# A two-layer trunk on one core: four kinds of store and two kinds of load change their issuing queue

## The chip, the cores and the metric

The kernel runs on one core of a Trainium2 chip. A core has TensorE (PE) for matmuls, VectorE (DVE), ScalarE (ACT) and GpSimd (POOL) for elementwise work, and SyncE (SP), which here only issues transfers. SP, ACT and POOL each have an instruction queue of their own that is worked off in order; a transfer that one of them issues moves between HBM and the on-chip memory while the queue goes on. The metric is the device time of one execution in microseconds (us), as a median of several runs.

## The reference, cut to what matters

The input `x` is 1024 positions by 1024 features in fp32. Two layers each hold a mixer and a feed-forward part. The mixer of layer 0 is a gated delta rule, that of layer 1 a retention.

```python
e = silu(c @ cond_w + cond_b)
for i in range(2):
    sh1, sc1, g1, sh2, sc2, g2 = split(e @ ada_w[i] + ada_b[i], 6)
    y = mixers[i](x * (1.0 + sc1) + sh1)          # gated delta rule, then retention
    x = layer_norm(ALPHA * x + (1.0 + g1) * y, ln_g[i, 0], ln_b[i, 0])
    gate, up = split((x * (1.0 + sc2) + sh2) @ ffn_up[i], 2)          # 1024 -> 2 x 2816
    y = (silu(causal_dwconv(gate, ffn_conv_w[i]) + ffn_conv_b[i]) * up) @ ffn_down[i]
    x = layer_norm(ALPHA * x + (1.0 + g2) * y, ln_g[i, 1], ln_b[i, 1])
```

## The kernel before, in words

Every fp32 product is made of three matmuls on rounded halves: `split` (L89, L90) has ACT copy a tile into a high part and DVE subtract it for the low part. The kernel works through these stages in time: delta rule with its projections (to about 700 us), first up projection (760 to 1160), first down projection (1160 to 1390), retention projections and core (1390 to 2070), its output projection (to 2210), second up projection (2210 to 2660) and second down projection (to the end).

The up projections work on eleven pairs of 128-column blocks, `fp` = 0 to 10, some 40 us each, with a matrix scheme that needs seven products in place of eight. For each of a pair's two items `wino` loads two weight tiles `wr` of 128 x 1024 (L1357, L1358; there are two buffers `wr`), builds differences of their halves on DVE (L1346), splits each half or difference into `wb`, and PE multiplies. ACT moves some sums off PSUM (`pc`, L1362). On the gate's result `conv_q` runs the causal convolution: an ACT copy (L1732), two DVE steps (L1737) and an ACT SiLU (L1738), into a tile `o`; then DVE multiplies by the up result (L1760). `store` (L1749) writes seven blocks per pair to `ad` in HBM: three as they are and four sums or differences, which POOL makes in place (L1768; DVE for `fp` = 0). There are 11 x 7 x 2 = 154 such stores of 256 KB. The `o` tiles are drawn from twenty half tiles `qkv`, of which the scheme holds sixteen here, so that a pair writes into the four tiles that the last pair stored from.

The down projections and retention's output projection are `proj_gen`: they read the seven blocks back as `ar` (L1425), load weight blocks as `Br` or `Bw` (`load_b`, L1458, 256 KB each, by the names "11", "21", "T1" to "T4"), split both into `ab` and `bb`, and add the residual rows `xt`, which `load_row` fetches (L296, 512 KB each; the first four rows belong to `half` 0, the last four to `half` 1). Br and ar share the `qkv` tiles. In the delta rule, `t_decay` stores eight decay matrices `Ld` of 512 KB (L842). In retention, `gain_step` writes sixteen scaled blocks `xg` of 256 KB back (L2052).

The order of each engine's queue is not the order of the code: the program is laid out by a scheduler that models when each instruction would be ready on its engine and queues them by that. `after(key)` only asks that an instruction is queued behind the one that `anchor[key]` holds. When a transfer moves to another engine, the queues of the others can thus change order too.

Of the kernel before, what the change touches and what calls it, by code (L numbers as in the profile page):

```python
# [15 lines left out]
P = 128  # L16
# [10 lines left out]
ABLK = ("11", "12", "22", "S1", "S2", "S3", "S4")  # L27
# [6 lines left out]
def trunk_kernel(ctx: ExitStack, tc, A):  # L34
    nc = tc.nc
    pe, act, dve, pool, sp = nc.tensor, nc.scalar, nc.vector, nc.gpsimd, nc.sync
# [9 lines left out]
    def tl(tag, shape, dt=F32, name=None):  # L46
        return sb.tile(shape, dt, tag=tag, name=name or tag, bufs=BUFS[tag])
# [31 lines left out]
    def flat(ap):  # L79
        return ap.rearrange("p a b -> p (a b)")  # L80

    def hs(half):
        return slice(half * HALF, (half + 1) * HALF)
# [8 lines left out]
    anchor = {}  # L92

    def after(key):
        return tc.issue_after(anchor[key].ins) if key in anchor else nullcontext()
# [84 lines left out]
    for k in range(KT):  # L180
        w = tl("hTa", [P, D], name="mvw")
# [107 lines left out]
    def build_hT(tag, xts, scale, shift, fr=range(KT)):  # L289
        return [build_one(tag, xts, scale, shift, f) for f in fr]  # L290

    def load_row(src, half, t, key=None, tag="lane"):
        xt = tl(tag, [P, D], name="xt")
        r0 = half * HALF + t * P
        with after(key), after("w" if key is None else None):
            sp.dma_start(xt, src[r0:r0 + P, :])  # L296
        return xt

    def mma(acc, t, a, w, first, last, mm):
# [91 lines left out]
    xg = [dr.tile([S, D], F32, tag=f"xg{i}", name=f"xg{i}") for i in range(3)]  # L391
# [229 lines left out]
    xt = [[tl("lane", [P, 2, HALF], name="xt") for _ in range(4)], [[None, None] for _ in range(4)]]  # L621
# [76 lines left out]
    U, DT, R, St = {}, {}, {}, {}  # L698
# [22 lines left out]
    def after_ev(*names):  # L721
        return ("ev", names)

    def emit(name, lat=0.0):
        events[name] = clk[0] + lat
# [45 lines left out]
    def take(tag, n):  # L771
        while free[tag] < n:
            yield lambda: free[tag] >= n
        free[tag] -= n
# [40 lines left out]
    Ld = dr.tile([GH, P, S], F32, tag="Ld", name="Ld")  # L815
# [17 lines left out]
    def t_decay(p):  # L833
        yield after_ev(("g",), ("DD", p - 1), ("T", p // 2 - 1))
        for h in pairs[p]:
            yield from take("aux", 1)
            U[h] = tl("aux", [P, NCH, P], name="U")
            yield from decay(h)
        yield LAT["mm"]
        for h in pairs[p]:  # L840
            act.activation(flat(U[h]), flat(U[h]), AF.Exp)
            sp.dma_start(Ld[h], flat(U[h]))  # L842
        emit(("DD", p), LAT["exp"])

    def t_path(g):
# [383 lines left out]
    c, z = "c", "z"  # L1229
# [5 lines left out]
    for p in range(4):  # L1235
        q = p & 2
# [192 lines left out]
    def proj_gen(nj, ablk, wsrc, slots, xsrc, G, final, ln_next, tag, ltags, dst, key, mm=pe.matmul, gate=None):  # L1429
# [8 lines left out]
        def keep(which, j):  # L1438
            t = slots[which]
            if t == "qkv":  # L1440
                return tl(t, [P, HALF], name="Bw")
            if j % 2 == 0:
                box[which] = tl(t, [P, 2, HALF], name="Bw")
            return box[which][:, j % 2]

        src = {"11": "11", "21": "21", "T1": "12", "T2": "22", "T3": "11", "T4": "21"}

        def load_b(bn, j):
            if bn not in src:
                return  # L1450
            if bn == "11":
                t = C[j] = keep("c", j)
            elif bn == "T2":
                t = X[j] = keep("x", j)
            else:
                t = R[bn, j] = tl("qkv", [P, HALF], name="Br")
            m = src[bn]
            anchor["w"] = sp.dma_start(t, wsrc[(m[1] == "2") * 1, j][:, hs((m[0] == "2") * 1)])  # L1458

        def bblk(bn, j):  # L1460
            if bn in ("11", "22"):
# [32 lines left out]
        def xload(half, t):  # L1494
            if half and t < 2:
                x = load_row(xsrc, half, t, tag="xT")
            elif half and final:
                x = two("auh", F32, "xt")
                r0 = HALF + t * P
                for hf in range(2):  # L1500
                    with after("w"):
                        sp.dma_start(x[hf], xsrc[r0:r0 + P, hs(hf)])
            else:
                x = load_row(xsrc, half, t)
            xts[half].append(x)
            stats[half].append(tl("st", [P, 2, 6]))

# [100 lines left out]
        for p, (an, bn, fin, side, fresh) in enumerate(prods):  # L1608
# [8 lines left out]
            for j in range(nj):  # L1617
# [4 lines left out]
                if (p, j) in ready:  # L1622
                    a, w = ready.pop((p, j))
                else:
                    a, w = ops(an, bn, j, not gate and p < (7 if final else 5))
# [3 lines left out]
                if not gate and p == 2 and j % 2 == 0 and j < 8:  # L1629
                    xload(0, j // 2)  # L1630
                if final and p == 3 and j % 2 == 0 and j < 8:
                    xload(1, j // 2)
# [48 lines left out]
    def layer_tail(i, mix, wout, xsrc, x_mid, x_out, ln_next, final):  # L1681
# [25 lines left out]
        ad = dr.tile([NF // 2, 7, P, HALF], F32, tag=f"ad{i}", name=f"ad{i}")  # L1707
# [4 lines left out]
        def pair_items(fp):  # L1712
            g, o = [], {}

            def gate_start():
                g.extend(tl("lane", [P, D], name="g") for _ in range(2))

                def gate(q, a, b):
                    dst = g[q // 2][:, hs(q % 2)]
                    if b is None:  # L1720
                        act.activation(dst, a, AF.Copy)
                    else:
                        dve.tensor_tensor(dst, a, b, ALU.add)
                return gate

            def conv_q(q):
                f, hf = 2 * fp + q // 2, q % 2
                gv = g[q // 2]
                w = cw[:, 3 * f:3 * f + 3]
                t = tl("qkv", [P, HALF], name="o")  # L1730
                with after("sp") if fp == 0 else nullcontext():
                    act.activation(t, gv[:, hs(hf)], AF.Copy, scale=w[:, 2:3])  # L1732
                for j in (1, 2):
                    c0 = HALF if hf else j
                    c1 = HALF * (hf + 1)
                    tv = t[:, c0 - HALF * hf:]
                    dve.scalar_tensor_tensor(tv, gv[:, c0 - j:c1 - j], w[:, 2 - j:3 - j], tv, ALU.mult, ALU.add)  # L1737
                act.activation(t, t, AF.Silu, bias=cb[:, f:f + 1])  # L1738
                o[q] = t

            def conv():
                for q in (1, 3, 0, 2) if fp == 0 else range(4):
                    if fp < 2:
                        late.append(lambda q=q: conv_q(q))
                    else:
                        conv_q(q)

            def store(nm, q):
                sp.dma_start(ad[fp, ABLK.index(nm)], o[q])  # L1749

            def up_start():
                seen = []

                def gated(q, a, b):
                    while q not in o:
                        late.pop(0)()
                    c = a
                    if b is not None:
                        dve.tensor_tensor(c, a, b, ALU.add)
                    dve.tensor_tensor(o[q], o[q], c, ALU.mult)  # L1760
                    if q != 1:
                        store({0: "11", 2: "12", 3: "22"}[q], q)
                    seen.append(q)
                    if len(seen) == 4:
                        for d, x, y, op, nm in ((1, 1, 3, ALU.add, "S1"), (0, 1, 0, ALU.subtract, "S2"),
                                                (2, 2, 0, ALU.subtract, "S4"), (3, 3, 0, ALU.subtract, "S3")):
                            def one(d=d, x=x, y=y, op=op, nm=nm):
                                (dve if fp == 0 else pool).tensor_tensor(o[d], o[x], o[y], op)  # L1768
                                store(nm, d)
                            if fp == 0:  # L1770
                                late.append(one)
                            else:
                                one()
                return gated

            return [(up[4 * fp], up[4 * fp + 2], gate_start, conv), (up[4 * fp + 1], up[4 * fp + 3], up_start, None)]
# [93 lines left out]
    for t in range(4):  # L1870
        x = tl("cv", [P, 516], name="xlo")[:, 0:HALF]
        r0 = HALF + t * P
# [174 lines left out]
    def gain_step(m):  # L2047
        if gx:
            x, c, rs, gb = gx.pop()
            pool.tensor_tensor(x, x, gb[0], ALU.mult)  # L2050
            pool.tensor_tensor(x, x, gb[1], ALU.add)
            sp.dma_start(xg[0][rs, hs(c)], x)  # L2052
        if m < 2 * NCH:
            c, r = divmod(m, NCH)
            if r == 0:
                gbs.append([tl("auh", [P, HALF], name="gb") for _ in range(2)])
                for t, nm in zip(gbs[-1], ("ln_g", "ln_b")):
                    sp.dma_start(t, A[nm][1:2, hs(c)].to_broadcast([P, HALF]))
            rs = slice(r * P, r * P + P)
            x = tl("lane", [P, HALF], name="xg")  # L2060
            sp.dma_start(x, xs[1][rs, hs(c)])
            gx.append((x, c, rs, gbs[-1]))
# [111 lines left out]
```

## Time and profile before

| | |
|---|---|
| median of 3 runs | 2893.8 us (2892.51 to 2897.38) |
| profiled execution | 2895.86 us, span 2894.1 us |
| mean granted TensorE clock | 0.989 |
| bytes moved | 465.30 MB, mean 161 GB/s |
| SP issues | 1278 transfers before, 1052 after |
| POOL issues | 33 transfers before, about 250 after |

A group's row in the profile names the line, the engine, the operation, the tiles written and read, their shape and the count, then busy time, mean time of one, and idle time of the engine just before with what ended it. A row of waits reads: who waited, for which engine and line, us in total, how often, and the longest. A row of the chain of waits gives start, length, engine, tile and line. SPq and PEld are SP's queue and PE's weight loads.

### The profile page before, as it was taken

To read this page: it belongs to the slowest core of one execution; us is meant where nothing else is said; L and a number is where in the kernel's file an instruction comes from. 1 tells how busy PE (TensorE), PEld (TensorE's weight loads), DVE (VectorE), ACT (ScalarE), POOL (GpSimd) and SP (SyncE) were. 2 spreads that over 40 slices of the span, in tenths; PEclk is the share of its full clock that TensorE was granted. 3 is DMA by queue.
4 is the path that set the end of the run, shared out by engine and by line. 5 is a ranking of instruction groups with operands and counts; after the bars stand their busy time and mean duration, and the time that the engine had idled before them with its cause. 6 is when DMAs were issued, how large, how long until landed. Compare 5 with 4: busy or idle time off the path is not lost.

```text
span 2894.1 us, 38921 instructions
## 1 busy us (share of the span) xinstructions
PE 2796.1 (97%) x13594; PEld 2287.9 (79%) x13594; DVE 2180.7 (75%) x3874; ACT 1295.6 (45%) x2387; POOL 487.1 (17%) x509
## 2 busy tenths in 40 slices
PE   8999999999999999999999999999999999999997
PEld 6787888877788778887888887777777788888886
DVE  5787688676788888868687656666688887777779
ACT  4663465344654444545333342222244644444543
POOL 0311221000023233000000002333201023332001
PEclk9999999999999999999999999999999999999999
DMA  7223243164254555855343364665754154434853
GB/s 277 88 95 121 91 137 99 52 240 153 95 189 164 193 182 171 295 154 189 126 148 120 120 200 151 198 207 172 245 195 146 62 197 138 142 129 164 289 182 117
DMA packets 252884, 465.30 MB, mean 161 GB/s; under 512 B 24144, under 2 KB 77776, under 8 KB 252688
## 3 DMA queue, kind: packets, MB, share of 16 engines
q1 hardware_dynamic: 218560, 408.02, 42.8%
q10 hardware_dynamic: 31488, 46.15, 4.3%
q0 software_dynamic: 2640, 8.65, 0.8%
q8 instruction: 107, 1.75, 0.3%
q14 instruction: 89, 0.73, 0.1%
HBM read 346.86 MB, written 115.87 MB: 160 GB/s over the span
## 4 chain that ended last, share of the span: by engine, by line
PE 54%; DVE 23%; DMA 12%; ACT 5%; issue 5%; POOL 1%; SPq 0%; ACTq 0%; DVEq 0%; POOLq 0%
PE acc L716 8%; PE acc L1292 5%; PE acc L1592 4%; PE acc L110 4%; PE acc L111 4%; PE acc L112 4%; PE sc L716 4%; DMA mvw<-in_ada_w 3%; PE sc L1292 3%; PE mm L716 2%; DVE o L1737 2%; DVE wb L90 2%; DMA wr<-in_ffn_up 2%; DVE qkv L490 2%; DVE mm L1346 2%
## 5 line engine op out<-in xcount | busy, mean ns | idle before, releaser
L716 PE MATMUL acc<-hT,wh 128*128 128x512 f32 x960 | 301.3, 396 | 0.0
L1592 PE MATMUL acc<-bb,ab 128*128 128x512 f32 x984 | 232.5, 396 | 7.1 <-DVE ab L90 3.7
L89 ACT ACTIVATE ab<-ar 128x512 fp32r<-128x512 f32 x210 | 131.1, 630 | 222.8 <-PE mm L303 49.8
L1592 PEld LDWEIGHTS acc<-bb,ab 128*128 128x128 f32 x984 | 185.6, 190 | 49.0 <-DVE bb L90 4.1
L716 PEld LDWEIGHTS acc<-hT,wh 128*128 128x128 f32 x960 | 183.7, 191 | 36.1
L90 DVE TENSOR_TENSOR ab<-ar,ab 128x512 fp32r<-128x512 f32 x210 | 147.8, 710 | 83.0 <-ACT ab L89 83.0
L1292 PE MATMUL acc<-T,wb 128*128 128x512 f32 x840 | 202.0, 390 | 0.4 <-DVE wb L90 0.4
L716 PE MATMUL acc<-hT,wl 128*128 128x512 f32 x480 | 197.9, 412 | 3.5 <-ACT sq L509 2.4
L89 ACT ACTIVATE wb<-mm 128x512 fp32r<-128x512 f32 x216 | 124.3, 597 | 169.5 <-DVE mm L1346 155.2
L1292 PEld LDWEIGHTS acc<-T,wb 128*128 128x128 f32 x840 | 157.6, 188 | 33.7 <-ACT o L1738 1.2
L90 DVE TENSOR_TENSOR wl<-wr,wh 128x1024 fp32r<-128x1024 f32 x98 | 124.6, 1272 | 76.5 <-ACT wh L89 72.8
L89 ACT ACTIVATE wh<-wr 128x1024 fp32r<-128x1024 f32 x98 | 103.6, 1060 | 138.3 <-PE acc L716 53.5
L90 DVE TENSOR_TENSOR wb<-wr,wb 128x512 fp32r<-128x512 f32 x162 | 115.8, 716 | 62.9 <-ACT wb L89 62.9
L1768 POOL TENSOR_TENSOR o<-o 128x512 f32<-128x512 f32 x80 | 113.4, 1426 | 267.4 <-ACT pc L1362 176.3
L1737 DVE SCALAR_TENSOR_TENSOR o<-g,vc,o 128x512 f32<-128x512 f32 (+2 forms) x176 | 149.6, 860 | 8.6 <-ACT o L1732 7.4
L90 DVE TENSOR_TENSOR wb<-mm,wb 128x512 fp32r<-128x512 f32 x216 | 145.2, 685 | 7.6 <-ACT wb L89 7.6
L89 ACT ACTIVATE wb<-wr 128x512 fp32r<-128x512 f32 x162 | 101.1, 626 | 92.7 <-PE acc L1292 27.9
L1346 DVE TENSOR_TENSOR mm<-wr 128x512 f32<-128x512 f32 x108 | 85.8, 794 | 74.5 <-DMA wr<-in_ffn_up 60.9
L716 PE MATMUL acc<-wh,hT 128*128 128x512 f32 x384 | 134.4, 412 | 1.8 <-DVE vv L90 1.8
L1362 ACT ACTIVATE pc<-acc 128x512 f32<-128x512 f32 x143 | 84.3, 590 | 108.7 <-PE acc L1292 63.0
L239 DVE SCALAR_TENSOR_TENSOR ada<-mvw,e,ada 128x512 f32<-128x512 f32 x140 | 106.0, 757 | 26.0 <-DMA mvw<-in_ada_w 25.7
L110 PE MATMUL acc<-T,wb 128*128 128x512 f32 x292 | 114.5, 392 | 5.2 <-DVE wb L90 5.1
(674 smaller groups left out, 7369.9 us busy)
## 6 DMA issues: line engine op xcount, KB each, us to landing
wr<-in_ffn_up SPq DMA_DIRECT2D x92, 512.0 KB, 3.9
mvw<-in_ada_w SPq DMA_DIRECT2D x80, 512.0 KB, 4.3
ad<-o SPq DMA_DIRECT2D x154, 256.0 KB, 2.3
ar<-ad SPq DMA_DIRECT2D x154, 256.0 KB, 3.8
Br<-in_ffn_down SPq DMA_DIRECT2D x88, 256.0 KB, 3.4
wr<-in_ret_wv SPq DMA_DIRECT2D x32, 512.0 KB, 3.6
ar<-od SPq DMA_DIRECT2D x56, 256.0 KB, 4.8
wr<-in_gdn_wqkv SPq DMA_DIRECT2D x24, 512.0 KB, 3.6
```

The lines of the kernel that those rows point to most:

```text
L89: anchor["sp"] = act.activation(dst_h, src, AF.Copy)
L90: eng.tensor_tensor(dst_l, src, dst_h, ALU.subtract)
L110: mm(acc, wl[:, k], hl[0], start=first, stop=False)
L111: mm(acc, wh[:, k], hl[1], start=False, stop=False)
L112: mm(acc, wh[:, k], hl[0], start=False, stop=last)
L239: dve.scalar_tensor_tensor(a, wr[:, kk], e[:, k:k + 1], a, ALU.mult, ALU.add)
L716: pq(pe.matmul(out, lhsT, rhs, start=start, stop=stop), cost or COST[out.shape[-1]])
L1292: return pe.matmul(*a, skip_group_check=True, **kw)
L1346: dve.tensor_tensor(t, x, y, op)
L1592: return pe.matmul(*args, skip_group_check=True, **kw)
L1737: dve.scalar_tensor_tensor(tv, gv[:, c0 - j:c1 - j], w[:, 2 - j:3 - j], tv, ALU.mult, ALU.add)
L1768: (dve if fp == 0 else pool).tensor_tensor(o[d], o[x], o[y], op)
```

## The change

Four kinds of store and two kinds of load get another issuer. The product stores `ad<-o` of both up projections and retention's `xg` stores go from SP to POOL, the `Ld` stores from SP to ACT. In the first down projection the weight blocks except "11" and "21" go from SP to POOL (43 transfers); they no longer set the anchor "w". Of the residual rows of the first down projection and of retention's output projection, the last two of `half` 1 go from SP to POOL (four transfers). All else stays on SP.

```diff
-    def load_row(src, half, t, key=None, tag="lane"):
+    def load_row(src, half, t, key=None, tag="lane", eng=sp):
...
-        with after(key), after("w" if key is None else None):
-            sp.dma_start(xt, src[r0:r0 + P, :])
+        with after(key), after("w" if key is None and eng is sp else None):
+            eng.dma_start(xt, src[r0:r0 + P, :])
...
-            sp.dma_start(Ld[h], flat(U[h]))
+            act.dma_start(Ld[h], flat(U[h]))
...
+            eng = sp if gate or final or bn in ("11", "21") else pool
...
-            anchor["w"] = sp.dma_start(t, wsrc[(m[1] == "2") * 1, j][:, hs((m[0] == "2") * 1)])
+            ld = eng.dma_start(t, wsrc[(m[1] == "2") * 1, j][:, hs((m[0] == "2") * 1)])
+            if eng is sp:
+                anchor["w"] = ld
...
-                x = load_row(xsrc, half, t)
+                x = load_row(xsrc, half, t, eng=pool if half else sp)
...
-                sp.dma_start(ad[fp, ABLK.index(nm)], o[q])
+                pool.dma_start(ad[fp, ABLK.index(nm)], o[q])
...
-            sp.dma_start(xg[0][rs, hs(c)], x)
+            pool.dma_start(xg[0][rs, hs(c)], x)
```

Below, lines of before from L1461 on carry a number that is 3 higher in the changed kernel: the conv copy L1732 is L1735 there, the conv steps L1737 are L1740, the SiLU L1738 is L1741, `store` L1749 is L1752, and L1458 is L1459.

VectorE in the pair of the first up projection that holds the load of 941.83 us, of which the prediction speaks; `wb<-mm` and `wb<-wr` are the subtractions of splits, the second one whose end frees a `wr` buffer. Before:

```order
L1346 TENSOR_TENSOR mm<-wr 128x512
L90 TENSOR_TENSOR wb<-mm,wb 128x512
L1723 TENSOR_TENSOR g<-acc,pc 128x512
L90 TENSOR_TENSOR wb<-mm,wb 128x512
L1737 SCALAR_TENSOR_TENSOR o<-g,vc,o 128x511
L1737 SCALAR_TENSOR_TENSOR o<-g,vc,o 128x510
L90 TENSOR_TENSOR wb<-wr,wb 128x512 x2
L1346 TENSOR_TENSOR mm<-wr 128x512
```

After:

```order
L1346 TENSOR_TENSOR mm<-wr 128x512
L90 TENSOR_TENSOR wb<-mm,wb 128x512
L1726 TENSOR_TENSOR g<-acc,pc 128x512
L90 TENSOR_TENSOR wb<-mm,wb 128x512
L90 TENSOR_TENSOR wb<-wr,wb 128x512
L1740 SCALAR_TENSOR_TENSOR o<-g,vc,o 128x511
L1740 SCALAR_TENSOR_TENSOR o<-g,vc,o 128x510
L90 TENSOR_TENSOR wb<-wr,wb 128x512
L1346 TENSOR_TENSOR mm<-wr 128x512
```

The first split of a half has moved ahead of the two conv steps; the second one stays behind them. ScalarE at the same place, before:

```order
L89 ACTIVATE wb<-mm 128x512 x2
L1732 ACTIVATE o<-g,vc 128x512
L1362 ACTIVATE pc<-sc 128x512
L89 ACTIVATE wb<-wr 128x512
L1738 ACTIVATE o<-o,vc 128x512
L1362 ACTIVATE pc<-acc 128x512
L89 ACTIVATE wb<-wr 128x512
```

After:

```order
L89 ACTIVATE wb<-mm 128x512 x2
L1362 ACTIVATE pc<-sc 128x512
L89 ACTIVATE wb<-wr 128x512
L1735 ACTIVATE o<-g,vc 128x512
L1362 ACTIVATE pc<-acc 128x512
L89 ACTIVATE wb<-wr 128x512
```

The conv copy has moved behind an eviction and a split, and the SiLU further down. GpSimd over one pair of the first up projection; `ad` is the store, L411 to L413 scale and store blocks of the residual. Before:

```order
L1768 TENSOR_TENSOR o<-o 128x512 x4
L411 TENSOR_TENSOR xg<-xg,gb 128x512
L412 TENSOR_TENSOR xg<-xg,gb 128x512
L413 DMA xg_161<-xg 128x512
```

After:

```order
L1752 DMA ad_6811<-o 128x512
L1771 TENSOR_TENSOR o<-o 128x512
L1752 DMA ad_6811<-o 128x512 x2
L1771 TENSOR_TENSOR o<-o 128x512
L1752 DMA ad_6811<-o 128x512
L1771 TENSOR_TENSOR o<-o 128x512 x2
L1752 DMA ad_6811<-o 128x512 x2
L411 TENSOR_TENSOR xg<-xg,gb 128x512
L412 TENSOR_TENSOR xg<-xg,gb 128x512
L413 DMA xg_161<-xg 128x512
```

Stores now stand between GpSimd's four steps. In the first down projection SP's queue around the two rows of `half` 1, before:

```order
L1425 DMA ar<-ad_6811 128x512
L1458 DMA Br<-in_ffn_down 128x512
L1425 DMA ar<-ad_6811 128x512
L1458 DMA Br<-in_ffn_down 128x512
L296 DMA xt<-xg_161 128x1024 x2
L1425 DMA ar<-ad_6811 128x512
L1458 DMA Br<-in_ffn_down 128x512
```

After:

```order
L1459 DMA Br<-in_ffn_down 128x512
L1425 DMA ar<-ad_6811 128x512 x12
L296 DMA xt<-xg_161 128x1024 x2
L1425 DMA ar<-ad_6811 128x512 x13
```

The Br loads that alternated with ar are gone from SP's queue; they stand in GpSimd's, fifteen of them in a row, behind the last stores of the up projection.

## The prediction

> **What bounds the kernel now.** I read the page first, then busy time by stage, then what TensorE (PE) and SyncE's queue (SPq) wait for in each stage, and the chain of waits around PE's stops. The page's engines:
>
> ```profile
> span 2894.1 us, 38921 instructions
> PE 2796.1 (97%) x13594; PEld 2287.9 (79%) x13594; DVE 2180.7 (75%) x3874; ACT 1295.6 (45%) x2387; POOL 487.1 (17%) x509
> ```
>
> PE is busy 97%: 2894.1 - 2796.1 = 98 us is all that can go without less PE work. The profiled execution took 2895.9 us (span 2894.1 and 1.8 around it), 0.07% above the median 2893.8 of the runs; I make the sum on its span and subtract from the median. About 0.2% of it, 5.8 us, is what a measurement here can tell from no change. Busy time by stage (columns PE, PEld, DVE, ACT, POOL, then granted clock, DMA share, GB/s; the stages: delta rule, first up projection, first down projection, second up projection):
>
> ```profile
> 0.00:700.00 700.00, 658.47 (x4158) 558.90 (x4159) 513.08 (x1183) 357.65 (x744) 115.03 (x175) 0.98 0.40 137
> 760.00:1160.00 400.00, 392.25 (x1724) 319.54 (x1725) 340.35 (x524) 193.46 (x379) 106.84 (x84) 1.00 0.50 171
> 1160.00:1390.00 230.00, 225.05 (x990) 184.61 (x989) 175.29 (x289) 114.63 (x197) 11.52 (x10) 0.99 0.62 208
> 2210.00:2660.00 450.00, 441.67 (x1939) 359.69 (x1938) 353.57 (x534) 216.15 (x364) 110.96 (x89) 0.99 0.40 135
> ```
>
> The change can reach PE's idle 400 - 392.3 = 7.7 us in the first up projection, 5.0 in the first down projection, 8.3 in the second up projection; the delta rule has the most, 41.5. What SPq waits for at the edited lines, over the span:
>
> ```profile
> SPq L1749 <- DVE o L1760: 215.9, 51, 9.7
> SPq L842 <- ACT U L841: 75.8, 8, 14.3
> SPq L1749 <- POOL o L1768: 57.8, 57, 3.7
> SPq L2052 <- POOL xg L2051: 43.3, 16, 6.3
> ```
>
> Together 393 us of a queue that stands still for a store, with loads behind it. That looks like much, but it only counts where such a load is what PE waits for. What PE waits for, in the first up projection, in the first down projection, and in the second up projection:
>
> ```profile
> PE acc L110 <- DVE wb L90: 5.1, 4, 1.5
> PE sc L110 <- DVE wb L90: 0.7, 2, 0.4
> ...
> PE acc L1592 <- DVE bb L90: 3.3, 1, 3.3
> ...
> PE acc L110 <- DVE wl L90: 4.2, 2, 3.2
> PE acc L1292 <- DVE wb L90: 1.0, 2, 0.8
> ```
>
> In the delta rule the longest behind the start is on ScalarE, so no store of the change ends it:
>
> ```profile
> PE acc L719 <- ACT oq L488: 5.3, 1, 5.3
> ```
>
> **The change, part by part.** *The seven product stores of a column pair (L1749, 154 in all) go from SP to POOL.* The chain up to one of the four stops on `wb` of L110, and ScalarE's queue at the same place:
>
> ```profile
> 938.05 0.61 DVE g L1723
> ...
> 938.74 0.73 ACT o L1732
> ...
> 939.50 0.93 DVE o L1737
> ...
> 941.11 0.70 DVE wb L90
> ...
> 941.83 5.80 DMA wr<-in_ffn_up
> 947.65 0.70 DVE mm L1346
> ```
>
> ```profile
> 939.37 0.57 ACT L1362 ACTIVATE pc<-sc 128x512 f32<-128x512 f32 x1
> 939.84 0.62 ACT L89 ACTIVATE wb<-wr 128x512 fp32r<-128x512 f32 x1
> ```
>
> The weight load of 941.83 was issued the moment its buffer came free: the split `wb<-wr` (ACT L89, then DVE L90) ended at 941.11 + 0.70 = 941.81. So SP's wait for stores does not delay it: freeing SP by itself is worth nothing here. But the split ran late: ahead of it stood the first conv copy (ACT, 0.73) and two conv steps (DVE, from 939.50 to 941.11). The new order puts the split ahead of the copy and of the two steps. DVE has `g` until 938.66 and one more split of 0.70 before it, until 939.4; ACT's half, without the copy ahead, is done 0.73 earlier, at 939.84 + 0.62 - 0.73 = 939.7. So DVE's half ends at about 939.7 + 0.7 = 940.4 in place of 941.81: some 1.4 us earlier. The four stops are 5.1 / 4 = 1.3 us on average, 1.5 at most. The DVE work behind the load stays the same, so an earlier load reaches PE nearly whole: I take 5.8 us (5.1 + 0.7) as gone, with 0 and 7.7 as ends. What is late next there: the load itself, 5.80 us, since DVE is busy 85% of this stage.
>
> What POOL pays: its issues are longer than SP's, and between them stand its own steps.
>
> ```profile
> L413 POOL DMA_DIRECT2D xg<-xg x32: 580/580/759, 837.2 to 2631.0; - x32
> ...
> DMA to landing us min/median/max: 2.3/2.3/5.5
> ...
> L1749 SPq DMA_DIRECT2D ad<-o x154: 319/320/1307, 790.2 to 2690.3; - x154
> ...
> DMA to landing us min/median/max: 2.0/2.3/6.2
> ...
> L1768 POOL TENSOR_TENSOR o<-o 128x512 f32<-128x512 f32 x36 | 51.2, 1432 | 91.7 <-ACT pc L1362 88.5 <-DMA ad<-o 1.6
> ```
>
> Seven stores at 0.58 add 4.1 us to POOL per pair. The stage's 400 us hold about ten pairs, so POOL's 106.8 us are 10.7 of 40 per pair: it goes to 15 of 40, no bound. A store lands 0 to 0.3 us later (medians 2.3 against 2.3, minima 2.3 against 2.0). It now stands behind POOL's own steps and POOL waits for VectorE's `o`, up to 9.7 us, with L1768's steps queued behind; who waits for that is the conv copy L1735 (before: L1732), which writes an `o` tile that the last pair stored from. That copy is moved behind a split (0.62 us) and an eviction (0.57), so 0.62 + 0.57 = 1.2 us of lateness is covered. I charge nothing, and take the end in the rival below. In the trace POOL's issues are steady: 32 of L413 lie at 580 ns median, 759 at most, in stages where DVE is busy 340.35 / 400 = 85% and 353.57 / 450 = 79%. The Trainium skill, "SBUF — State Buffer", section "SBUF: two separate sides", in its box on VectorE blocking a DMA, says that GpSimd cannot write descriptors while VectorE holds the shared port pair, and gives 620 ns alone against some 3100 beside such a step; by that, an estimate, a store comes up to 2.5 us later, past the cover of 1.2, and rival B would be the result. By that rule L413's issues should scatter up to microseconds, and the trace does not agree.
>
> *The same stores in the second up projection:* the same move; what can go is the 1.0 us on `wb` of L1292. I take 1.0, ends 0 and 2.
>
> *First down projection: 43 weight blocks on POOL, the rest on SP.* The chain to its stop of 3.3 us, and SP's queue there:
>
> ```profile
> 1307.62 4.39 DMA ar<-ad
> ...
> 1312.77 2.79 DMA Br<-in_ffn_down
> ...
> 1316.97 3.18 DMA Br<-in_ffn_down
> ```
>
> ```profile
> 1307.62 0.32 SPq L1425 DMA_DIRECT2D ar<-ad  x1
> 1312.77 0.33 SPq L1458 DMA_DIRECT2D Br<-in_ffn_down  x1
> 1313.20 0.86 SPq L296 DMA_DIRECT2D xt<-xg  x2
> ```
>
> Loads go out as buffers come free: the one of 1312.77 had its tile released at that moment. On POOL each issue is 0.26 us longer (580 - 320) and lands up to 0.3 later, so two steps on the chain cost 2 x 0.3 to 0.6 = 0.6 to 1.1 us. Against this, SP stood in that wait from 1307.94 to 1312.77, and behind it were two residual rows of 512 KB (1313.20), which then shared the engines with both Br loads; now they are free to go in the pause. Two windows of this stage, and one from 2230:
>
> ```profile
> 1310.00:1330.00 20.00, 16.71 (x71) 13.43 (x70) 14.31 (x25) 4.48 (x8) 0.00 (x0) 0.96 0.41 132
> 1370.00:1390.00 20.00, 20.00 (x85) 16.42 (x84) 14.87 (x25) 3.42 (x4) 0.56 (x1) 0.93 0.43 152
> 2230.00:2245.00 15.00, 11.81 (x40) 9.17 (x39) 7.67 (x14) 3.23 (x4) 1.94 (x2) 0.77 0.39 144
> ```
>
> The granted clock is below 1 there (0.96, 0.93), which costs 0.04 x 20 + 0.07 x 20 = 2.2 us beside the 3.3 idle. The stage's ends are thus -5.5 (both gone) and +3 (1.1 more of stop, and the 2.2 of clock nearly once more); the two are opposed and I see no reason to prefer one, so I take 0.
>
> *Two late residual rows of each of two projections (L296) on POOL.* In the first down projection they are needed long after. Before the second up projection they are on the chain:
>
> ```profile
> 2223.94 4.44 DMA xt<-xg
> ```
>
> What lies behind it is the 3.2 us stop on `wl` and a clock of 0.77 over 15 us. Two issues at 0.58 in place of 0.86 / 2 = 0.43 and up to 0.3 in landing: 0 to +0.6; I take +0.5, since the landing is the larger part and nothing covers it.
>
> *Ld stores on ACT (L842), retention's xg stores on POOL (L2052).* Eight issues, at the 0.32 of SP above, are 2.6 us on an ACT busy 51% in that stage; SP gets 75.8 us of waiting back, but the PE stops there are ACT's own. Sixteen issues at 0.58 are 9.3 us on POOL, which is busy 17% of the span; SP gets 43.3 back. I take 0 for both, ends -2 and +2.
>
> **Sum:** -5.8 - 1.0 + 0 + 0.5 + 0 = -6.3 us: 2893.8 - 6.3 = 2887.5, which I round to 2887.
>
> **The rivals.** *A, nothing measurable.* The wr load takes 5.8 us however early it starts, since stores and loads now crowd together, and the splits that are earlier meet the same data. For: the bytes are unchanged and the chain says wr, not SP. Against: DMA share is 0.50, so room is there. Then 0 to -3: 2892. The Trainium skill, "DMA: Bandwidth & Descriptors", section "Issuing engines are not separate DMA queues", says the same in general: DMAs of every issuer share 16 engines, and several issuers save only issue time. By that rule A is the result.
>
> *B, slower: the conv copy waits for POOL's queue.* In order, ACT stops at L1735 until the store of the last pair has been issued by POOL, and behind it stand all splits of the weights. It decides when the first stores of a pair come more than the 1.2 us of cover later than on SP; one POOL step of L1768 (1432 ns) ahead of one would do. With 11 pairs in each up projection, 20 of them behind another, and half of 1.2 us each reaching PE: 20 x 0.6 = 12, and nothing gained: 2893.8 + 12 = 2906, from 2900 on for a part of the pairs. For: SP's waits show POOL as releaser at 57 of the stores, so they do stand close behind POOL's steps. Against: POOL is idle 73% of that stage.
>
> *C, a larger gain.* The 3.3 us stop of the first down projection and the clock behind it go: 2887.5 - 5.5 = 2882. For: the pause in SP's issues from 1307.94 to 1312.77. Against: the tiles, not SP, release the Br loads.
>
> **How the numbers follow.** Forecast 0.45 (2883 to 2892), A 0.17, B 0.23, C 0.15. Faster by over 5.8 us: C 0.15 and 0.29 of the forecast's 0.45: 0.44. Within 5.8 (0.2%): the other 0.16, A's 0.14, B's 0.02: 0.32. Slower: B 0.21 and A 0.03: 0.24. The range reaches down to C with 4 us of unknown in the delta rule and retention (2877) and up to B with half of its pairs struck, 2900, and 3 of the down projection (2903).
>
> **What would show it.** Right: PE's waits on `wb` L90 in the first up projection under 2 us, the wr load issued before 941 in the same pair, SPq with no wait at the stores. Wrong: ACT waiting at L1735 for a DMA of POOL; POOL issues well over 0.6 us; PE idle over 8 us in 1160 to 1390; a clock below 0.7 in the 15 us after 2230.

## The result, and the profile after

The changed kernel took 2908.0 us (median of 6 runs, 2901.0 to 2910.7) against 2893.2 of the kernel before beside it: a ratio of 1.0042, interval 1.0027 to 1.0056. In a second comparison it was 1.0040 (1.0021 to 1.0058). By the ratio it is slower by about 12 us, and its median lies 5 us beyond the upper end of the forecast range; the forecast had been 6 us faster. Its profiled execution took 2908.6 us. The page's head and engines:

```profile
span 2906.8 us, 38823 instructions
PE 2798.1 (96%) x13594; PEld 2285.8 (79%) x13594; DVE 2206.8 (76%) x3874; ACT 1294.3 (45%) x2387; POOL 602.4 (21%) x727
```

PE's work is the same. VectorE, with the same 3874 instructions, is busy 26.1 us longer (2206.8 - 2180.7): some of its steps have become slower. By stage, for the first up projection and the second one (to 2660):

```profile
760.00:1160.00 400.00, 392.15 (x1721) 318.04 (x1720) 349.69 (x523) 193.57 (x382) 139.74 (x154) 1.00 0.51 170
...
2210.00:2660.00 450.00, 436.60 (x1913) 353.84 (x1912) 356.28 (x525) 210.74 (x355) 147.66 (x161) 0.99 0.40 134
```

What SP waited for, in the lines that answer to those of before (no wait stands at the stores of L1752 and L2055, or at L842), before and then after:

```profile
SPq L1358 <- DVE wb L90: 85.9, 50, 5.1
```

```profile
SPq L1358 <- DVE wb L90: 217.9, 51, 6.8
```

SP is free of the stores, as intended, and waits at the weight loads instead: these need a buffer that a split releases. PE's waits in the first up projection and the second one:

```profile
PE acc L110 <- DVE wb L90: 4.1, 4, 1.6
PE sc L110 <- DVE wb L90: 1.6, 2, 1.3
...
PE sc L1292 <- DVE ada L239: 2.5, 1, 2.5
PE acc L1292 <- ACT pc L1362: 1.6, 3, 0.5
```

The 5.8 us that should have gone are still 5.7 (4.1 + 1.6), and in the second up projection a stop of 2.5 us is new. Which of VectorE's steps got slower shows when shapes are kept apart: first the splits `wb<-wr` of the second up projection before, then after, then splits and `ada` steps of the first up projection before, then after.

```profile
L90 DVE TENSOR_TENSOR wb<-wr,wb 128x512 fp32r<-128x512 f32 x60 | 42.3, 706 | 17.3 <-ACT wb L89 17.3
```

```profile
L90 DVE TENSOR_TENSOR wb<-wr,wb 128x512 fp32r<-128x512 f32 x59 | 53.2, 905 | 17.5 <-ACT wb L89 17.5
```

```profile
L90 DVE TENSOR_TENSOR wb<-wr,wb 128x512 fp32r<-128x512 f32 x59 | 43.9, 746 | 11.0 <-ACT wb L89 11.0
L239 DVE SCALAR_TENSOR_TENSOR ada<-mvw,e,ada 128x512 f32<-128x512 f32 x56 | 43.1, 770 | 0.0
```

```profile
L90 DVE TENSOR_TENSOR wb<-wr,wb 128x512 fp32r<-128x512 f32 x59 | 57.4, 975 | 10.1 <-ACT wb L89 10.1
L239 DVE SCALAR_TENSOR_TENSOR ada<-mvw,e,ada 128x512 f32<-128x512 f32 x56 | 49.6, 886 | 0.1
```

The new stop of 2.5 us in the chain of waits, then GpSimd at that place:

```profile
2374.62 0.63 ACT wb L89
...
2375.28 2.72 DVE wb L90
...
2378.02 6.33 DMA wr<-in_ffn_up
```

```profile
2372.72 1.30 POOL L1771 TENSOR_TENSOR o<-o 128x512 f32<-128x512 f32 x1
2374.32 0.56 POOL L1752 DMA_DIRECT2D ad<-o  x1 [0.30 <-POOL o L1771]
2374.90 2.53 POOL L1771 TENSOR_TENSOR o<-o 128x512 f32<-128x512 f32 x2
```

The split starts at 2375.28, inside two sums that GpSimd works back to back from 2374.90 to 2377.43, and it ends at 2378.00, when they are over: 2.72 us in place of 0.70. The weight load that waits for its buffer goes out at 2378.02, two microseconds late. The chains at two of the stops of about 0.5 us behind it begin in the same way:

```profile
2456.27 2.44 DVE wb L90
2458.73 4.20 DMA wr<-in_ffn_up
...
2572.97 1.85 DVE wb L90
2574.83 4.07 DMA wr<-in_ffn_up
```

Each load leaves when a stretched split ends. In the first up projection three stops, at 882.5, 923.3 and 1083.3, hold 4.5 of the 5.7 us, and their chains begin so as well, with splits of 2.59, 2.85 and 2.73 us; the first:

```profile
865.53 2.59 DVE wb L90
...
868.14 4.26 DMA wr<-in_ffn_up
```

To compare stages over kernels whose clocks and starts differ, the table gives the time between the same two matmuls of PE's queue (by their number in the queue), those that start at 770, 1160, 1290, 1390, 2200, 2250 and 2660 us in the kernel before. Kernels whose code is alike in a stage scatter there by 3 us in the first up projection (389.3 to 392.3) and by 0.8 in the second (409.4 to 410.2).

| kernel | first up 770-1160 | first down 1290-1390 | 2200-2250 | second up 2250-2660 | ratio to before |
|---|---|---|---|---|---|
| before | 390.0 | 100.1 | 49.8 | 410.2 | |
| changed | 390.6 | 96.9 | 50.5 | 415.6 | 1.0042 |
| changed, again | 392.3 | 95.9 | 50.5 | 416.3 | 1.0040 |
| e1 product stores alone | 390.0 | 97.5 | 45.5 | 415.2 | 1.0007 |
| e2 Ld alone | 389.3 | 98.8 | 48.7 | 409.4 | 0.9997 |
| e3 down blocks and rows alone | 392.3 | 96.3 | 47.6 | 409.9 | 0.9987 |
| e4 xg alone | 389.7 | 97.2 | 45.5 | 409.7 | 0.9991 |
| e6 all but the product stores | 391.4 | 97.0 | 47.6 | 409.4 | 0.9995 |
| e7 changed, sums on VectorE | 380.0 | 96.1 | 49.2 | 408.0 | 0.9975 |
| e7b before, sums on VectorE | 385.0 | 101.1 | 49.7 | 408.2 | 0.9974 |
| e11 e7 with fills on GpSimd | 379.9 | 99.3 | 50.5 | 414.2 | 0.9994 |
| e12 the best | 380.4 | 96.5 | 45.3 | 408.7 | 0.9943 |
| e13 changed, rows on SyncE | 391.8 | 97.3 | 48.6 | 413.2 | 1.0029 |
| e8 S stores on SyncE | 393.2 | 95.6 | 46.8 | 409.2 | 0.9997 |

The four stages do not hold the whole loss: from before to changed they add up to 3.5 us, of 12.7 between the two profiled executions. Counted in the same way, the stretch up to 770 goes from 770.1 to 774.9, but the five kernels that keep before's code in the delta rule and are not before itself take 773.2 to 778.9 there, so nothing can be read from it. The stretch from 1390 to 2200 goes from 810.0 to 812.5 and, in the repeat, 813.2; the others take 806.6 to 811.5, and no run shows whether the change costs something there.

### The profile page after: what moved, and what is told of

The parts are those of the page before. It is cut to its first block, busy times and chain, and to the rows that moved or that the text cites. A ratio compares the mean times of both kernels' runs of the same rounds, so it can differ in the third digit from the quotient of the medians.

```text
span 2906.8 us, 38823 instructions
## 1 busy us (share of the span) xinstructions
PE 2798.1 (96%) x13594; PEld 2285.8 (79%) x13594; DVE 2206.8 (76%) x3874; ACT 1294.3 (45%) x2387; POOL 602.4 (21%) x727
## 4 chain that ended last, share of the span: by engine, by line
PE 56%; DVE 21%; DMA 10%; issue 7%; ACT 5%; POOL 1%; SPq 0%; ACTq 0%; DVEq 0%; POOLq 0%
PE acc L716 8%; PE acc L1292 6%; PE acc L110 5%; PE acc L111 5%; PE acc L112 5%; PE sc L716 3%; PE sc L1292 3%; PE mm L716 3%; DVE wb L90 2%; DMA wr<-in_ffn_up 2%; DVE qkv L490 2%; PE acc L1595 2%; DMA mvw<-in_ada_w 2%; PE sc L110 2%; PE sc L111 2%
## 5 line engine op out<-in xcount | busy, mean ns | idle before, releaser
L1595 PEld LDWEIGHTS acc<-bb,ab 128*128 128x128 f32 x984 | 183.2, 188 | 47.3 <-DVE ab L90 2.8
L90 DVE TENSOR_TENSOR wb<-wr,wb 128x512 fp32r<-128x512 f32 x162 | 140.8, 871 | 62.0 <-ACT wb L89 62.0
L1752 POOL DMA_DIRECT2D ad<-o x154 | 84.4, 549 | 415.4 <-DVE o L1763 397.8
L1740 DVE SCALAR_TENSOR_TENSOR o<-g,vc,o 128x512 f32<-128x512 f32 (+2 forms) x176 | 136.0, 783 | 9.7 <-ACT o L1735 8.2
L239 DVE SCALAR_TENSOR_TENSOR ada<-mvw,e,ada 128x512 f32<-128x512 f32 x140 | 116.1, 829 | 25.0 <-DMA mvw<-in_ada_w 24.5
L1346 DVE TENSOR_TENSOR mm<-wr 128x512 f32<-128x512 f32 x108 | 81.5, 755 | 62.9 <-DMA wr<-in_ffn_up 49.7
L110 PE MATMUL acc<-T,wb 128*128 128x512 f32 x292 | 114.7, 393 | 4.7 <-DVE wb L90 4.6
```

The source lines that it names most:

```text
L90: eng.tensor_tensor(dst_l, src, dst_h, ALU.subtract)
L110: mm(acc, wl[:, k], hl[0], start=first, stop=False)
L239: dve.scalar_tensor_tensor(a, wr[:, kk], e[:, k:k + 1], a, ALU.mult, ALU.add)
L1595: return pe.matmul(*args, skip_group_check=True, **kw)
L1752: pool.dma_start(ad[fp, ABLK.index(nm)], o[q])
```

## The experiments

**Each part alone.** The edits are those of the change's diff, one at a time.

> Only the 154 product stores go to GpSimd; all else as before. Theory 1 (the loss sits in the up projections: stores between GpSimd's sums push these onto VectorE's splits, and ScalarE's conv copy waits for stores): +6 to +8 us, 2899 to 2901, with L90 wb<-wr at a mean near 0.9 us in both up projections in place of 0.75 and 0.71. Theory 2 (the loss sits in the delta rule, by ScalarE issuing the Ld stores, and in retention): 0 to +2 us. The forecast on record, for this part alone: -7.

Measured: 1.0007 (0.9994 to 1.0019). The second up projection takes 415.2 us, 5 more than before, with splits at a mean of 903 ns; the first takes 390.0. So the product stores carry the loss of the second up projection, and none that shows in the first. The total is lower than expected because 4.3 us come back in 2200 to 2250, for a reason of its own: PE's queue there has two orders. In one (before, changed, e2, e7, e7b, e11, e13) the last transposes stand eleven matmuls later in PE's queue, and the stage takes 48.6 to 50.5 us; in the other (e1, e3, e4, e6, e8, e12) 45.3 to 47.6. Which one the scheduler picks can change with an edit elsewhere.

> Only the eight Ld stores go to ScalarE. Theory 1: 0 to +2 us (the +5 us that the changed kernel's trace has in the delta rule is mostly order by chance). Theory 2: +4 to +5 us, all before 650 us.

Measured: 0.9997 (0.9981 to 1.0012). No cost that these runs could tell.

> Only the 43 weight blocks of the first down projection and the four late residual rows go to GpSimd. Theory 1: -3 us in 1280 to 1390 (the trace of the changed kernel gains 3 there) and up to +0.7 at the rows before the second up projection: 2891. Theory 2 says the same of this part; a third theory, that every transfer on GpSimd's queue costs time, says +1 to +3.

Measured: 0.9987 (0.9973 to 1.0002). 1290 to 1390 is 96.3 us. (The blocks are 44 by the trace, 33 into `Br` and 11 into `Bw`, not 43.) Kernels with the blocks on SyncE have 97.2 to 101.1 there, those with them on GpSimd 95.6 to 99.3: means 98.9 and 96.8, so some 2 us gained. No cost of GpSimd's queue as such.

> Only retention's sixteen xg stores go to GpSimd. Theory 1: 0 to +1 us. Theory 2: +2 to +3 us between 1750 and 2080.

Measured: 0.9991 (0.9978 to 1.0003), with the favourable order at 2200 (45.5). The rest is within the scatter.

**The changed kernel again, and without the product stores.**

> The changed kernel again, on the chip of the other experiments. Compared at the same granted clock, the parts alone measured +5.9 (product stores), +1.0 (Ld), -0.9 (down blocks and rows), -1.0 (xg): if the parts add, +5 us; if the parts act on each other, +10 as in the first comparison.

Measured: 1.0040 (1.0021 to 1.0058): as at first. The parts alone add to -0.2% by their ratios, partly because three of them (e1, e3, e4) fell into the favourable order at 2200, worth 2 to 4 us each, and the whole did not.

```diff
-                pool.dma_start(ad[fp, ABLK.index(nm)], o[q])
+                sp.dma_start(ad[fp, ABLK.index(nm)], o[q])
```

> The changed kernel with the 154 product stores back on SyncE. If the product stores are the cost: -3 to +1 us against before, and 409.5 us for the second up projection (before 410.2, changed kernel 415.6). If other parts or their interplay hold half of it: +4 to +5.

Measured: 0.9995 (0.9979 to 1.0010), second up projection 409.4. With the 154 product stores back on SyncE the loss is gone, and the other parts are worth about nothing together. Of the 13 us between this kernel and the changed one, the second up projection holds 6 to 7 and the other order at 2200 holds 2.8; 3 to 4 lie between 1390 and 2200, unexplained.

**Taking GpSimd's sums away.**

```diff
-                                (dve if fp == 0 else pool).tensor_tensor(o[d], o[x], o[y], op)
+                                dve.tensor_tensor(o[d], o[x], o[y], op)
```

> The changed kernel with GpSimd's four sums per pair (L1771) on VectorE, so that only stores and the xg steps are left on GpSimd there. VectorE gets 4 x 0.69 = 2.8 us per pair more. Theory 1 (the cost is VectorE's split that stands beside GpSimd's sums): the splits wb<-wr are back at about 0.70 us mean in the second up projection, from 0.91, and this kernel differs from the one with the same sums on VectorE and stores on SyncE by under 2 us in the second up projection. Rival (the cost is the in-order queue of GpSimd: ScalarE's conv copy waits for stores): the difference stays at 5 us.

> The kernel before with GpSimd's four sums per pair on VectorE, stores on SyncE: the control for the run beside it. Both theories: the splits at 0.70 us; the second up projection between 409 (no collisions left) and 416 (VectorE loaded by 2.8 us more per pair).

Measured: 0.9975 (0.9963 to 0.9988) and 0.9974 (0.9961 to 0.9988): both faster than before, though VectorE got 80 more steps. In the second up projection they are alike, 408.0 and 408.2, so the stores on GpSimd cost nothing there once the sums are elsewhere. In the first up projection stores on GpSimd gain 5 us (380.0 against 385.0): 3.1 of it at two places, the rest in steps of 0.3 us or less, and no run shows the cause. It is not the new order of VectorE's queue: in the first up projection the split stands ahead of both conv steps in nine pairs of the changed kernel, but in one of e7 and none of e7b. In the second it does in eight of the changed kernel, seven of e7 and none of e7b: there, with the sums away, the new order neither costs nor gains. The splits and PE's waits of the kernel with the stores on GpSimd, in the first up projection:

```profile
L90 DVE TENSOR_TENSOR wb<-wr,wb 128x512 fp32r<-128x512 f32 x60 | 42.2, 705 | 15.2 <-ACT wb L89 15.1
PE acc L1292 <- DVE wb L90: 1.2, 2, 1.0
```

All stops of L110 on `wb` are gone. But two things went with the sums: the stretched splits, and the lateness of stores behind sums in GpSimd's queue.

**Lateness without stretching.**

```diff
-                                (dve if fp == 0 else pool).tensor_tensor(o[d], o[x], o[y], op)
+                                anchor["sum"] = dve.tensor_tensor(o[d], o[x], o[y], op)
+                                if fp:
+                                    with after("sum"):
+                                        for _ in range(2):
+                                            pool.memset(tl("t2", [P, HALF]), 0.0)
```

> As the run with the sums on VectorE and stores on GpSimd, but GpSimd gets two fills of a spare 128x512 tile per sum as a stand-in, which read no memory; they do nothing for the result. Theory 1 (GpSimd steps that read memory beside VectorE's splits are the cost): if the trace shows the splits at 0.70 us beside the fills, the second up projection stays at 408 to 409 us. Rival (a busy in-order GpSimd queue, whose stores come late for ScalarE's conv copy): it goes back to 413 to 416 with splits at 0.70. If the fills lengthen the splits too, the run cannot tell the two apart.

Measured: 0.9994 (0.9983 to 1.0005). The splits stay short (699 ns in the second up projection), the first up projection stays at 379.9, but the second goes to 414.2. There GpSimd and then VectorE read:

```profile
2553.95 3.82 POOL L1775 MEMSET t<- 128x512 f32 x8
2557.70 2.13 POOL L1752 DMA_DIRECT2D ad<-o  x4
```

```profile
2562.86 1.29 DVE L1771 TENSOR_TENSOR o<-o 128x512 f32<-128x512 f32 x2 [3.19 <-DMA ad<-o]
2564.07 0.69 DVE L90 TENSOR_TENSOR wb<-wr,wb 128x512 fp32r<-128x512 f32 x1
```

Eight fills of 3.82 us hold up four stores, VectorE's sum waits 3.19 us for one of these before it may overwrite the tile, and the split stands behind it. So lateness in GpSimd's queue by itself can cost as much as stretching. It does not show that it did so in the changed kernel.

```diff
-                pool.dma_start(ad[fp, ABLK.index(nm)], o[q])
+                (sp if nm[0] == "S" else pool).dma_start(ad[fp, ABLK.index(nm)], o[q])
```

> The changed kernel with the four stores of sums per pair (S1 to S4) back on SyncE and the three direct ones left on GpSimd: an o tile is now free when SyncE has stored it, not when GpSimd's queue gets to it, while GpSimd's sums still run behind issues of stores. If the stretched splits are enough: ScalarE's waits for stores at the conv copy under 5 us per up projection, splits beside GpSimd's steps still at 1.3 us or more, and 413 to 416 us for the second up projection. If the lateness of stores in GpSimd's queue is what counts: 408 to 410 us whatever the splits do.

Measured: 0.9997 (0.9984 to 1.0011); second up projection 409.2, the first 393.2. ScalarE waited 7.4 us for stores in the second, and the splits are in between too, 777 ns:

```profile
L90 DVE TENSOR_TENSOR wb<-wr,wb 128x512 fp32r<-128x512 f32 x60 | 46.5, 777 | 14.9 <-ACT wb L89 14.8
```

With four of seven issues gone from GpSimd, both effects shrink together. VectorE's order went back too: the split stands ahead of both conv steps in one pair of each up projection, in place of nine and eight. So this run does not separate the two.

**The rows, and the best version.**

```diff
-                x = load_row(xsrc, half, t, eng=pool if half else sp)
+                x = load_row(xsrc, half, t)
```

> The changed kernel with the four late residual rows back on SyncE. PE's order around them is that of the changed kernel. If the rows cost what the landing times say (5.1 to 5.5 us against 4.4): 0.7 us less in 2200 to 2250 (49.8 in place of 50.5), +10 to +11 us against before. If the rows make up the 5 us by which the changed kernel is slower than the product stores alone: +6.

Measured: 1.0029 (1.0015 to 1.0042), 2200 to 2250 in 48.6 us against 50.5. Over all kernels, rows on GpSimd take 50.2 against 49.2 us in the one order (means of four each) and 47.3 against 45.4 in the other (three each): 1 to 2 us. The first estimate, 0.7, was low; the rows do not make up 5 us.

The best version takes the product stores and down blocks of the change, the sums on VectorE, and leaves Ld, xg and the rows on SyncE:

> The product stores and the down projection's weight blocks on GpSimd, the sums on VectorE, and Ld, xg and the residual rows on SyncE as before. If the stage times of the earlier traces add: first up projection 380 us (before 390), second 408 (410.2), 1290 to 1390 96 (100 in the profile of before, 97 to 101 in others of that order), 2200 to 2250 45.5 (49.8) because this kernel queues PE's last transposes earlier: -14 to -18 us, 2880. If those single profiles misled: -7, as the other two with the sums on VectorE.

Measured: 2881.3 us, 0.9943 (0.9930 to 0.9956): by the ratios 16 us faster than before and 28 faster than the changed kernel. The stage times added. Some 4 of the 16 us come from the favourable order at 2200, which no edit asks for. PE's waits in 2225 to 2245, where the stop was 3.2 us before:

```profile
PE acc L110 <- DVE wl L90: 1.6, 1, 1.6
```

## Why the prediction was wrong

**The failed step** is the one that let VectorE's half of the split, moved ahead, end "at about 939.7 + 0.7". The 0.70 us came from a row of before, where that split stood behind the conv steps and clear of GpSimd. In the changed kernel it does not. The same split, the load behind it, and GpSimd beside it:

```profile
946.87 2.37 DVE L90 TENSOR_TENSOR wb<-wr,wb 128x512 fp32r<-128x512 f32 x1 [1.61 <-ACT wb L89]
```

```profile
949.27 5.54 DMA wr<-in_ffn_up
```

```profile
941.05 0.54 POOL L1752 DMA_DIRECT2D ad<-o  x1
941.61 1.30 POOL L1771 TENSOR_TENSOR o<-o 128x512 f32<-128x512 f32 x1
942.84 1.09 POOL L1752 DMA_DIRECT2D ad<-o  x2
943.95 1.31 POOL L1771 TENSOR_TENSOR o<-o 128x512 f32<-128x512 f32 x1
945.56 0.56 POOL L1752 DMA_DIRECT2D ad<-o  x1 [0.30 <-POOL o L1771]
946.13 2.55 POOL L1771 TENSOR_TENSOR o<-o 128x512 f32<-128x512 f32 x2
```

The changed kernel is 6.9 us behind at this place (the same PE matmul starts at 938.65 before and at 945.52 here). So the split does start 1.1 us earlier than before, but the load leaves 0.6 us later, in place of the 1.4 us earlier of the prediction. Four store issues (0.54 + 1.09 + 0.56 = 2.2 us) stand ahead of the last two sums, which run from 946.13 to 948.68. They push these back onto the split, which had moved ahead to meet them. Beside such sums, six splits in the first up projection and seven in the second take over 1 us, up to 2.96. Before, no split does: there fourteen conv steps and eleven half-differences (L1346) take over 1 us beside the sums, up to 1.87. Two terms failed so: -5.8 in the first up projection measured +0.6 and +2.3 in the two traces, no change within the scatter of 3 us, and -1.0 in the second measured +5.5 and +6.1. At the place of the example PE's stop still became 1.0 us shorter, as steps behind the load changed their order too; it is at the stops named under the result that PE lost time.

**Whether the order gains by itself stays open.** No kernel here has the new order in most pairs of the first up projection without GpSimd's sums, so nothing shows whether -5.8 would have come. With a split of 0.70 the load of the example would have left 1.1 us earlier (an estimate from its start, 946.87); the rest of the 1.4 was missing because the eviction ahead of ScalarE's half waited for PE's sum. The prediction did not look at its condition, that GpSimd is quiet at that place.

**Rival B** had the sign, and the size (+12) by luck: it charged both up projections alike, and only the second lost. ScalarE does wait for GpSimd's stores at the conv copy, in the first up projection:

```profile
ACT o L1735 <- issue: 20.7, 6, 4.4
...
ACT o L1735 <- DMA ad<-o: 17.3, 11, 2.4
```

Before, the copy was L1732:

```profile
ACT o L1732 <- DMA ad<-o: 5.4, 5, 2.8
...
ACT o L1732 <- issue: 2.9, 1, 2.9
```

That is 8.3 us before and 38.0 after, in a stage that did not get slower beyond its scatter. In the chains that begin at 2374, 2456 and 2572, ScalarE's half of the split comes ahead of the copy that waits, so what released the load late was VectorE's half. That the waits cost something elsewhere is not excluded; how the loss divides between stretching and lateness stays open, since no kernel here had the one without the other beside GpSimd's sums.

**The rule that was weighed** was the wrong part of the right section. POOL's issues stayed at 548 ns in the second up projection, as the trace of before had said. But a store landed 3.3 us after its issue at the median, where it had been 2.3 from SyncE and the prediction took 0 to 0.3 more (2.8 with the sums on VectorE); no run shows what holds it up. Before, then after:

```profile
ad<-o SPq DMA_DIRECT2D x154, 256.0 KB, 2.3
```

```profile
ad<-o POOLq DMA_DIRECT2D x154, 256.0 KB, 3.3
```

The Trainium skill, "SBUF — State Buffer", section "SBUF: two separate sides", also says there that a VectorE step with two SBUF inputs and a GpSimd step that reads SBUF lock each other out for a whole instruction. The trace agrees: in the second up projection of the changed kernel's repeat, splits of two SBUF tiles beside GpSimd's steps take 1.42 us on average and up to 2.68, those beside its DMA issues 0.69, and splits whose one input is in PSUM (`wb<-mm`) 0.68 beside either. The split at 2375.28 waited through two sums in a row, which is more than one whole instruction.

**The rest.** The first down projection was put at 0 and gained about 2 us. The rows were put at +0.5 and cost 1 to 2. Ld and xg were put at 0 and showed nothing beyond the scatter. That SP's waits are worth nothing by themselves held: SP lost all its waits at stores, and got them back at the weight loads.

## What to carry to other kernels

A duration taken from a trace holds for the neighbours that the instruction has there: when a change moves a step, or moves what another engine does beside it, look up who will now run at the same time before its old duration is used. Before transfers go to an engine's queue, look at that engine's other work: each issue pushes its steps, and each step pushes its transfers, and someone waits for both. When parts are measured one by one, look at stages as well as totals, and at whether the queues still have the order in question; an unrelated place where the scheduler flips between two orders can hide 4 us.

## What the runs showed of the hardware that had not been expected

In these traces GpSimd's sums delay splits whose two inputs both lie in SBUF and not those with one input in PSUM, by up to the whole rest of a back-to-back pair (2.72 us for a step of 0.70, at 2375.28), while a DMA issue on GpSimd, at 0.55 us, delays none. Which of the two starts first decides: in the second up projection of the changed kernel a split that began 0.12 us ahead of a GpSimd step took 0.68 us (2386.84), one that began 0.01 us behind the start of a sum 1.84 (2495.94). Fills on GpSimd delay none either: in the run with fills the nine splits beside them took 0.70 us. Moving 80 sums to VectorE, at 0.69 us each where GpSimd took 1.3 to 1.4, made the kernel faster by 0.26% although VectorE is the busier engine.
